# Moving the gain of the MLP's first norm from the rows of w_up to the transposed h, in a one-core decoder layer

## The chip, the core and the metric

The kernel runs on one core of one Trainium2 chip. The metric is the device time of one execution in microseconds (us). Besides DMA queues the core has five engines that matter here: PE (matmuls and transposes, which write to PSUM), ACT (ScalarE), DVE (VectorE), POOL (GpSimd) and SP (which issues most DMAs). Each engine works through its own queue in order, and waits on semaphores for the others.

## The reference

One decoder layer on x of 256 tokens by 2048 channels, in fp32. Two attention groups give `mixed`, and then:

```python
x = x + _rmsnorm(mixed @ w_out[layer], norm_attn_post[layer])

h = _rmsnorm(x, norm_mlp_pre[layer])
u = jnp.square(jax.nn.relu(h @ w_up[layer]))
x = x + _rmsnorm(u @ w_down[layer], norm_mlp_post[layer])
```

`_rmsnorm(x, gain)` divides each token's row by its root mean square and multiplies channel c by `gain[c]`. The gain of the MLP's first norm, `norm_mlp_pre`, multiplies the contraction index of `h @ w_up`; it can therefore be applied either to the channels of h or to the rows of w_up. w_up is 2048 x 8192 and w_down 8192 x 2048.

## The kernel before, in words

**Precision.** Every large matmul is done in three passes. An operand `a` is split into `hi` (a rounded to the matmul's format, written by an ACT copy) and `lo` (`a - hi`, written by DVE), and hi·hi + hi·lo + lo·hi is accumulated. `split` (L290) does this with an ACT copy and a DVE subtraction; `split_gain` (L296) does the same on `g * a`, where `g` is one number per partition: ACT takes it as its scale, DVE uses a SCALAR_TENSOR_TENSOR (multiply, then subtract) in place of a TENSOR_TENSOR. Both engines read the source, and DVE also reads the `hi` that ACT has just written.

**Tiling.** The contraction index lies on the 128 partitions, in tiles k of 128 rows. The tokens are two blocks b of 128. A weight tile is 128 x 1024 columns; it is loaded by DMA into one of five `raw` buffers and split into `hi` and `lo` (eight buffers each) several tiles ahead of its use (`Weights.emit`, L178). `wide_u` (L401) plans the tiles of w_up: 16 k-tiles for the first chunk of 1024 columns (j = 0), and for each of the seven further chunks 10 plain k-tiles and three pairs of k-tiles that are done in seven block products instead of eight, from sums of blocks of weights (`seven`, L333) and of h (`left_sums`, L958). The gains of the rows of w_up lie in `gcol`, one column per k-tile (columns 8 to 23). The plain k-tiles (16 + 7 x 10 = 86) are split with their column of `gcol`; the pairs are not multiplied by it, and there `left_sums` multiplies h instead.

**The stage around the change.** Out-projection (`acc_o`) ends with the fourth chunk of 512 columns, first for block b = 0, then for b = 1. When a block is finished, `residual(b)` (L832) runs beside the matmuls. It computes the token's scale (DVE, then POOL), updates x in four pieces of 512 channels on DVE (L841), and for each piece n lets PE transpose four 128 x 128 blocks into one PSUM tile `ht` (L847 to L849). The four `ht` tiles of a block take the two PSUM banks of `tp_bank` (L275) in turn, so that the third piece's transposes write the bank of the first, and the fourth's the bank of the second. Then `split` turns all four blocks of the PSUM tile at once into `hT_hi` and `hT_lo` (L853, one ACT and one DVE instruction of 128 x 512). After the four pieces x is sent to DRAM by a DMA on SP (L856), and ACT sums the squares of x (L860).

The matmuls of the first chunk of w_up (`acc_u`) begin while this is under way: k-tiles 0 to 6 for b = 0, then 0 to 6 for b = 1, then both blocks for each later k-tile. PE's queue holds them and the transposes in one fixed order. The order of all work is written out by `Flow`, a clock of assumed costs that decides between which matmuls each step of `residual` is placed; splits of weight tiles fall between the splits of h on ACT and DVE.

`left_sums` (L958) runs after that, for three pairs of k-tiles. It adds hT_hi and hT_lo, multiplies by the gain (L965), forms the block sums, and splits both the multiplied h (back into hT) and the sums.

Below, k-tiles of w_up in the first chunk are called k0, k1 and so on, and the pieces of h n0 to n3 of block b0 or b1.

## Time and profile before

| | us |
|---|---|
| median of three runs | 1053.56 (1052.34 to 1053.63) |
| profiled execution | 1052.05 |
| its span, first to last instruction | 1050.3 |
| PE busy in it | 1039.0 |
| DVE busy | 811.0 |
| ACT busy | 625.4 |
| POOL busy | 61.5 |

The span is what the profile sees between its first and last instruction; 1.75 us of the profiled execution's time lie around it. The views used are: the page's first part (busy time by engine), the list of waits of PE, groups of instructions by line and shape (count, busy time, mean duration), and the instructions of one engine in order of time. In such a time row the columns are start, duration, engine, line, operation, output <- inputs, shapes and count; a bracket at the end gives the idle time before it and what ended it. Durations of neighbours on one engine overlap a little (about 0.1 us on ACT and 0.06 to 0.1 on DVE), so the distance between starts is the time that an instruction costs its queue.

### The profile page before, as it was taken

The numbers are of one execution on the slowest core, as the hardware profiler recorded it, in microseconds if no ns is written. First come the engines' busy times: TensorE is split into PE (matmuls) and PEld (weight loads), VectorE is DVE, ScalarE is ACT, GpSimd is POOL, SyncE is SP. The second block draws the span as 40 slices with busy tenths as digits, with TensorE's granted clock in tenths as the row PEclk, the third lists the DMA queues.
The fourth block names the chain that finished last, engine by engine and source line by source line (L and its number), as shares of the span: only waits on it lengthen the run. The fifth ranks groups of instructions, "written<-read, shape, count | busy, mean of one in ns | idle before, by whom it ended". The sixth has DMA issues, their size and how long they took to land.

```text
span 1050.3 us, 13459 instructions
## 1 busy us (share of the span) xinstructions
PE 1039.0 (99%) x4854; PEld 865.9 (82%) x4854; DVE 811.0 (77%) x1080; ACT 625.4 (60%) x834; POOL 61.5 (6%) x116
## 2 busy tenths in 40 slices
PE   9999999999999999999999999999999999999996
PEld 6888899888888788888888888888888888888885
DVE  6676536577557679879888798887899978989995
ACT  6675436565555467666665666666567564766661
POOL 0000000000000000010000000000000001112100
PEclk9999999999999999999999999999999999999999
DMA  8975447454447295646556465469788767788952
GB/s 298 371 230 155 140 127 239 141 166 155 141 170 234 77 344 174 224 143 238 194 189 201 145 234 194 151 227 319 246 276 315 267 223 259 268 300 313 381 186 81
DMA packets 80643, 229.34 MB, mean 218 GB/s; under 512 B 7616, under 2 KB 12224, under 8 KB 80192
## 3 DMA queue, kind: packets, MB, share of 16 engines
q1 hardware_dynamic: 65888, 176.45, 50.3%
q0 software_dynamic: 14112, 51.39, 14.2%
q8 instruction: 38, 0.62, 0.2%
q10 hardware_dynamic: 576, 0.64, 0.2%
q14 instruction: 29, 0.24, 0.1%
HBM read 212.72 MB, written 15.73 MB: 218 GB/s over the span
## 4 chain that ended last, share of the span: by engine, by line
PE 96%; DVE 1%; DMA 1%; issue 1%; ACT 0%; POOL 0%; DVEq 0%; POOLq 0%; ACTq 0%
PE y L283 26%; PE acc_u L283 26%; PE acc_o L283 8%; PE m L283 5%; PE md L283 5%; PE acc_v L283 4%; PE acc_qk L283 4%; PE acc_ckv L283 2%; PE acc_ukv L283 2%; PE acc_q L283 2%; PE acc_cq L283 2%; PE acc_k L283 2%; PE acc_uq L283 2%; PE rt L287 1%; PE sc_b L283 1%
## 5 line engine op out<-in xcount | busy, mean ns | idle before, releaser
L294 DVE TENSOR_TENSOR lo<-raw,hi 128x1024 fp32r<-128x1024 f32 (+3 forms) x213 | 241.7, 1152 | 91.5 <-ACT hi L293 90.7
L293 ACT ACTIVATE hi<-raw 128x1024 fp32r<-128x1024 f32 (+3 forms) x213 | 209.5, 999 | 77.6 <-PE y L283 20.8
L283 PE MATMUL acc_u<-hi,hT_hi 128*128 128x512 f32 x386 | 153.3, 397 | 0.0
L283 PE MATMUL acc_u<-hi,hT_lo 128*128 128x512 f32 x386 | 151.0, 391 | 0.4 <-DVE hT_lo L294 0.4
L283 PE MATMUL acc_u<-lo,hT_hi 128*128 128x512 f32 x386 | 150.7, 391 | 0.0
L283 PE MATMUL y<-hi,uhi 128*128 128x512 f32 x376 | 146.8, 390 | 0.0
L283 PE MATMUL y<-hi,ulo 128*128 128x512 f32 x376 | 146.5, 390 | 0.0
L283 PE MATMUL y<-lo,uhi 128*128 128x512 f32 x376 | 146.5, 390 | 0.0
L298 DVE SCALAR_TENSOR_TENSOR lo<-raw,gcol,hi 128x1024 fp32r<-128x1024 f32 x86 | 107.6, 1280 | 11.2 <-ACT hi L297 11.0
L297 ACT ACTIVATE hi<-raw,gcol 128x1024 fp32r<-128x1024 f32 x86 | 97.8, 1151 | 24.8 <-PE acc_u L283 10.9
L283 PEld LDWEIGHTS acc_u<-hi,hT_lo 128*128 128x128 f32 x386 | 72.5, 188 | 16.1 <-DVE hT_lo L294 0.8
L283 PEld LDWEIGHTS acc_u<-lo,hT_hi 128*128 128x128 f32 x386 | 72.6, 188 | 14.2
L283 PEld LDWEIGHTS acc_u<-hi,hT_hi 128*128 128x128 f32 x386 | 72.6, 188 | 13.9
L283 PEld LDWEIGHTS y<-hi,uhi 128*128 128x128 f32 x376 | 70.6, 188 | 14.6
L283 PEld LDWEIGHTS y<-hi,ulo 128*128 128x128 f32 x376 | 70.6, 188 | 14.6
L283 PEld LDWEIGHTS y<-lo,uhi 128*128 128x128 f32 x376 | 70.6, 188 | 14.5
L283 PE MATMUL acc_o<-hi,mixT_hi 128*128 128x512 f32 x128 | 51.9, 405 | 0.0
L294 DVE TENSOR_TENSOR lo<-st_down,hi 128x1024 fp32r<-128x1024 f32 x40 | 48.1, 1220 | 4.0 <-ACT hi L293 3.8
L283 PE MATMUL acc_o<-hi,mixT_lo 128*128 128x512 f32 x128 | 50.2, 392 | 0.0
L283 PE MATMUL acc_o<-lo,mixT_hi 128*128 128x512 f32 x128 | 50.0, 391 | 0.0
L293 ACT ACTIVATE hi<-ab 128x512 fp32r<-128x512 f32 (+1 forms) x38 | 32.0, 842 | 29.3 <-PE acc_u L283 24.4
L293 ACT ACTIVATE hi<-st_down 128x1024 fp32r<-128x1024 f32 x40 | 42.1, 1053 | 11.1 <-PE y L283 9.5
(322 smaller groups left out, 1986.3 us busy)
## 6 DMA issues: line engine op xcount, KB each, us to landing
raw<-in_w_down SPq DMA_DIRECT2D x88, 512.0 KB, 6.0
raw<-in_w_up SPq DMA_DIRECT2D x86, 512.0 KB, 4.5
raw<-in_w_in SPq DMA_DIRECT2D x55, 512.0 KB, 5.0
ab<-in_w_up POOLq DMA_DIRECT2D x36, 512.0 KB, 5.0
raw<-in_w_out SPq DMA_DIRECT2D x32, 512.0 KB, 4.3
ab_down<-in_w_down POOLq DMA_DIRECT2D x20, 512.0 KB, 6.4
ukeep<-ulo SPq DMA_DIRECT2D x15, 512.0 KB, 7.2
ulo<-ukeep POOLq DMA_DIRECT2D x15, 512.0 KB, 5.4
```

What stands on the lines that cost most here:

```text
L283: nc.tensor.matmul(out, a, b, start=start, stop=stop)
L287: nc.tensor.transpose(out, a, ident)
L293: nc.scalar.activation(hi, src, AF.Copy)
L294: nc.vector.tensor_tensor(out=lo, in0=src, in1=hi.bitcast(F32), op=OP.subtract)
L297: nc.scalar.activation(hi, src, AF.Copy, scale=g)
L298: nc.vector.scalar_tensor_tensor(out=lo, in0=src, scalar=g, in1=hi.bitcast(F32), op0=OP.mult, op1=OP.subtract)
```

## The change

Three edits. The plain k-tiles of w_up are split without the gain. In `residual`, the split of one `ht` tile becomes four calls of `split_gain`, one for each of its k-tiles, with that k-tile's column of `gcol`. In `left_sums`, where h now carries the gain already, the multiplication and the second split of h are left out; only the block sums are split.

```diff
@@ wide_u @@
             if what == "k":
-                ts = [weights.plan(up_weight(j, k), 1, CW, gcol[:, 8 + k:9 + k])]
+                ts = [weights.plan(up_weight(j, k), 1, CW)]
@@ residual @@
             if n in (0, 1):
                 update((n + 2,))
-            split(hT[0][:, 4 * n:4 * n + 4, b * P:(b + 1) * P], hT[1][:, 4 * n:4 * n + 4, b * P:(b + 1) * P], tv)
+            for k in range(4 * n, 4 * n + 4):
+                split_gain(*[tok(x, k, b) for x in hT], tv[:, k - 4 * n], gcol[:, 8 + k:9 + k])
@@ left_sums @@
-        for i in range(2):
-            nc.vector.tensor_scalar_mul(f[:, i * S:(i + 1) * S], f[:, i * S:(i + 1) * S], gcol[:, 8 + k + i:9 + k + i])
         four_sums(q, f)
         st = [late["st"][:, i * 512:(i + 1) * 512] for i in (2 * kp, 2 * kp + 1)]
         yield 3.0
-        for t, x in ((hs, f), (st, q)):
-            nc.scalar.activation(t[0], x, AF.Copy)
+        nc.scalar.activation(st[0], q, AF.Copy)
         yield 1.5
-        for t, x in ((hs, f), (st, q)):
-            tt(out=t[1], in0=x, in1=t[0].bitcast(F32), op=OP.subtract)
+        tt(out=st[1], in0=q, in1=st[0].bitcast(F32), op=OP.subtract)
```

The order on PE, POOL and SP is the same in both kernels. What moves is seen on ACT and DVE in the stage of the splits of h. The rows below are the queue's order, with the semaphores that a row waits for in brackets; `ht` is the PSUM tile of transposes, `hi` and `raw` are weight tiles.

ACT's queue before, from the first split of b0 to the fourth:

```order
L293 ACTIVATE hT_hi<-ht_3222 128x4x128 [waits PE_49]
L297 ACTIVATE hi_3235<-raw_3233,gcol 128x1024 [waits DMAHW7_49,DVE_49]
L293 ACTIVATE hT_hi<-ht_3242 128x4x128 [waits PE_49]
L802 ACTIVATE junko_3253,ssy_2434<-acc_o_0_1_0_3094 128x512 [waits PE_49,Activation_49]
L297 ACTIVATE hi_3262<-raw_3260,gcol 128x1024 [waits DMAHW0_49,DVE_49]
L293 ACTIVATE hT_hi<-ht_3269 128x4x128 [waits PE_49]
```

The same place now:

```order
L297 ACTIVATE hT_hi<-ht_3222,gcol 128x128 [waits PE_49]
L297 ACTIVATE hT_hi<-ht_3222,gcol 128x128 [waits DVE_49] x3
L293 ACTIVATE hi_3241<-raw_3239 128x1024 [waits DMAHW7_49]
L297 ACTIVATE hT_hi<-ht_3248,gcol 128x128 [waits PE_49]
L297 ACTIVATE hT_hi<-ht_3248,gcol 128x128 [waits DVE_49] x3
L802 ACTIVATE junko_3265,ssy_2434<-acc_o_0_1_0_3094 128x512 [waits PE_49,Activation_49]
L293 ACTIVATE hi_3274<-raw_3272 128x1024 [waits DMAHW0_49]
```

One instruction became four in the same place, and the second to fourth of them wait for DVE, which no split of h did before.

DVE's queue before, from the splits of b0 to the first updates of x for b1:

```order
L294 TENSOR_TENSOR hT_lo<-ht_3222,hT_hi 128x4x128 [waits Activation_49]
L298 SCALAR_TENSOR_TENSOR lo_3236<-raw_3233,gcol,hi_3235 128x1024 [waits DMAHW7_49,Activation_49]
L841 SCALAR_TENSOR_TENSOR x_117<-yg_2861,rstd_post_3196,x_117 128x512
L294 TENSOR_TENSOR hT_lo<-ht_3242,hT_hi 128x4x128 [waits Activation_49]
L803 TENSOR_TENSOR yg_2862<-acc_o_0_1_0_3094,g_post 128x512 [waits Activation_49]
L298 SCALAR_TENSOR_TENSOR lo_3263<-raw_3260,gcol,hi_3262 128x1024 [waits DMAHW0_49,Activation_49]
L294 TENSOR_TENSOR hT_lo<-ht_3269,hT_hi 128x4x128 [waits Activation_49]
```

The same place now:

```order
L298 SCALAR_TENSOR_TENSOR hT_lo<-ht_3222,gcol,hT_hi 128x128 [waits Activation_49] x4
L294 TENSOR_TENSOR lo_3242<-raw_3239,hi_3241 128x1024 [waits DMAHW7_49,Activation_49]
L841 SCALAR_TENSOR_TENSOR x_117<-yg_2861,rstd_post_3196,x_117 128x512
L298 SCALAR_TENSOR_TENSOR hT_lo<-ht_3248,gcol,hT_hi 128x128 [waits Activation_49] x4
L803 TENSOR_TENSOR yg_2862<-acc_o_0_1_0_3094,g_post 128x512 [waits Activation_49]
L294 TENSOR_TENSOR lo_3275<-raw_3272,hi_3274 128x1024 [waits DMAHW0_49,Activation_49]
L298 SCALAR_TENSOR_TENSOR hT_lo<-ht_3281,gcol,hT_hi 128x128 [waits Activation_49] x4
```

Each of the four waits for its own ACT instruction; the updates of x and the splits of weights stand behind them in the queue, in the order of before.

## The prediction

> **What bounds the kernel now.** I read the page's busy times first, then the list of PE's waits.

> ```profile
> span 1050.3 us, 13459 instructions
> PE 1039.0 (99%) x4854; PEld 865.9 (82%) x4854; DVE 811.0 (77%) x1080; ACT 625.4 (60%) x834; POOL 61.5 (6%) x116
> ```

> ```profile
> PE acc_qk L283 <- ACT hi L293: 1.0, 2, 0.8
> PE acc_u L283 <- DVE hT_lo L294: 0.4, 1, 0.4
> ```

> PE is busy for 99% of the span, and after the first microseconds it waits for a split once: 0.4 us for `hT_lo`, in the stage that is changed. So time saved on ACT or DVE elsewhere has nothing to win, and what counts is whether the changed stage makes PE wait. Its rows on PE, in order of time:

> ```profile
> 354.86 0.60 PE L287 MATMUL ht<-ident,x 128*128 128x128 f32 x4
> 356.69 0.60 PE L287 MATMUL ht<-ident,x 128*128 128x128 f32 x4
> 361.94 0.39 PE L283 MATMUL acc_u<-hi,hT_hi 128*128 128x512 f32 x1
> 363.07 0.39 PE L283 MATMUL acc_u<-hi,hT_lo 128*128 128x512 f32 x1
> 363.35 0.42 PEld L287 LDWEIGHTS ht<-ident,x 128*128 128x128 f32 x4 [0.31 <-issue]
> 363.38 0.63 PE L287 MATMUL ht<-ident,x 128*128 128x128 f32 x4
> 366.72 0.50 PE L283 MATMUL acc_u<-hi,hT_lo 128*128 128x512 f32 x1 [0.40 <-DVE hT_lo L294]
> 367.75 0.60 PE L287 MATMUL ht<-ident,x 128*128 128x128 f32 x4
> 369.58 0.60 PE L287 MATMUL ht<-ident,x 128*128 128x128 f32 x4
> 379.57 0.39 PE L283 MATMUL acc_u<-hi,hT_hi 128*128 128x512 f32 x1
> ```

> These are the third and fourth transposes of b0, the first use of k5, the last matmul before b1's transposes, the first transposes of b1, the first use of b1's `hT_lo`, b1's third and fourth transposes, and k8. Matmuls start 0.23 us apart (363.07 would be followed at 363.30; the load row before b1's transposes shows 0.31 us of idle time, which ends as the first of the two updates of x at 362.48 does, half of 1.41 us later). The queues beside it, DVE, and then ACT with one DMA of SP:

> ```profile
> 352.47 0.69 DVE L294 TENSOR_TENSOR hT_lo<-ht,hT_hi 128x512 fp32r<-128x512 f32 x1 [1.25 <-ACT hT_hi L293]
> 353.51 1.28 DVE L298 SCALAR_TENSOR_TENSOR lo<-raw,gcol,hi 128x1024 fp32r<-128x1024 f32 x1 [0.35 <-ACT hi L297]
> 354.71 0.74 DVE L841 SCALAR_TENSOR_TENSOR x<-yg,rstd_post,x 128x512 f32<-128x512 f32 x1
> 355.38 0.68 DVE L294 TENSOR_TENSOR hT_lo<-ht,hT_hi 128x512 fp32r<-128x512 f32 x1
> 355.98 0.68 DVE L803 TENSOR_TENSOR yg<-acc_o,g_post 128x512 f32<-128x512 f32 x1
> 360.16 1.28 DVE L298 SCALAR_TENSOR_TENSOR lo<-raw,gcol,hi 128x1024 fp32r<-128x1024 f32 x1
> 362.48 1.41 DVE L841 SCALAR_TENSOR_TENSOR x<-yg,rstd_post,x 128x512 f32<-128x512 f32 x2 [0.67 <-POOL rstd_post L485]
> 365.98 0.68 DVE L294 TENSOR_TENSOR hT_lo<-ht,hT_hi 128x512 fp32r<-128x512 f32 x1
> ```

> ```profile
> 351.84 0.60 ACT L293 ACTIVATE hT_hi<-ht 128x512 fp32r<-128x512 f32 x1 [4.45 <-PE ht L287]
> 354.43 0.60 ACT L802 ACTIVATE junko<-acc_o 128x512 bf16<-128x512 f32 x1 [0.17 <-PE acc_o L283]
> 361.61 1.15 ACT L297 ACTIVATE hi<-raw,gcol 128x1024 fp32r<-128x1024 f32 x1 [1.03 <-DMA raw<-in_w_up]
> 355.91 0.39 SPq L175 DMA_DIRECT2D raw<-in_w_up  x1
> ```

> The stretch before b1 in sum (columns: length, then busy us of PE, PEld, DVE, ACT and POOL):

> ```profile
> 356.00:362.00 6.00, 6.00 (x30) 4.97 (x29) 5.77 (x9) 4.93 (x10) 0.11 (x1) 1.00 0.78 262
> ```

> DVE is busy for 5.77 of these 6 us, up to the chain that makes x of b1 (362.48), and that chain already holds PE for 0.3 us. Whatever is added to DVE's queue here goes straight to PE.

> **Price of the new splits.** The same code (`split_gain` out of a PSUM tile that holds several pieces) stands in the latents' part:

> ```profile
> 180.52 0.45 ACT L297 ACTIVATE mixT_hi<-ckvt,gcol 128x256 fp32r<-128x256 f32 x1
> 181.53 0.84 ACT L297 ACTIVATE mixT_hi<-ckvt,gcol 128x256 fp32r<-128x256 f32 x2 [0.55 <-DVE mixT_lo L298]
> ```

> ```profile
> 181.01 0.48 DVE L298 SCALAR_TENSOR_TENSOR mixT_lo<-ckvt,gcol,mixT_hi 128x256 fp32r<-128x256 f32 x1 [0.19 <-ACT mixT_hi L297]
> 182.03 0.88 DVE L298 SCALAR_TENSOR_TENSOR mixT_lo<-ckvt,gcol,mixT_hi 128x256 fp32r<-128x256 f32 x2 [0.54 <-ACT mixT_hi L297]
> ```

> The second ACT piece of a tile does not follow the first: it waits 0.55 us, until DVE has read the tile's first piece. The two engines alternate, 1.01 us for a pair (180.52 to 181.53). In the changed order the second to fourth piece of each `ht` wait for DVE just so. For the width of 128 I take the slopes of these groups (columns: count, busy us, mean ns):

> ```profile
> L298 DVE SCALAR_TENSOR_TENSOR lo<-raw,gcol,hi 128x1024 fp32r<-128x1024 f32 x86 | 107.6, 1280 | 11.2 <-ACT hi L297 11.0
> L298 DVE SCALAR_TENSOR_TENSOR mixT_lo<-ckvt,gcol,mixT_hi 128x256 fp32r<-128x256 f32 x4 | 1.8, 481 | 1.3 <-ACT mixT_hi L297 1.3
> L297 ACT ACTIVATE hi<-raw,gcol 128x1024 fp32r<-128x1024 f32 x86 | 97.8, 1151 | 24.8 <-PE acc_u L283 10.9 <-DMA raw<-in_w_up 6.7 <-PE acc_o L283 3.1
> L297 ACT ACTIVATE mixT_hi<-ckvt,gcol 128x256 fp32r<-128x256 f32 x4 | 1.8, 467 | 1.1 <-DVE mixT_lo L298 1.1
> L294 DVE TENSOR_TENSOR lo<-raw,hi 128x1024 fp32r<-128x1024 f32 x179 | 215.8, 1222 | 69.7 <-ACT hi L293 69.0
> L293 ACT ACTIVATE hi<-raw 128x1024 fp32r<-128x1024 f32 x179 | 186.6, 1055 | 56.9 <-PE y L283 20.8 <-DMA raw<-in_w_in 11.0 <-PE acc_o L283 5.5
> ```

> DVE: (1280 - 481) / 768 = 1.04 ns a column, so 481 - 133 = 0.35 us for 128. ACT: (1151 - 467) / 768 = 0.89, so 467 - 114 = 0.35; with 0.04 us for each hand-over (180.52 + 0.45 to 181.01) a pair is 0.79 us (0.36 + 0.35 + 0.08). A group of four takes 4 x 0.79 - 0.04 = 3.1 us from ACT's start to DVE's end, where before it was 1.32 (351.84 to 353.16), and DVE is held for 3 x 0.79 + 0.35 = 2.7 us, where it was 0.6 (355.38 to 355.98). Bounds: a pair is no dearer than the 256-wide one (1.01), and no cheaper than with both pieces at half of their 256-wide rows (0.23 + 0.24 + 0.08 = 0.55). I take 0.79, by the slopes of both rows, which leave 0.21 and 0.24 us that do not depend on the width.

> **The sum, on before's clock.** I carry ACT's and DVE's queues forward in the new order, with a weight split at 1.05 and 1.22 us (the plain rows above), and note where PE must wait.

> - b0 n0: ACT begins at 351.9, DVE ends at 355.0. PE's third transposes, due at 354.86, write the same bank: **+0.2**.
> - ACT splits k3 from 354.5 to 355.6, DVE to 356.8; x's update to 357.5; only then DVE takes n1, which ends at 357.4 + 2.7 = 360.15. PE's fourth transposes (356.69 + 0.2 = 356.9) need n1's bank: **+3.3**.
> - `junko`, k4's split and `yg` follow; n2 runs on DVE from 362.5 to 365.2. ACT splits k5 from 364.7 to 365.75, DVE to 367.0. PE wants k5 at 361.94 + 3.5 = 365.4: **+0.4** for `hi`, **+1.0** for `lo`.
> - n3 on DVE to 369.6. k6's `lo` begins at 370.25. From there to x's first update for b1 it took 362.48 - 360.16 = 2.3, so it begins at 372.45 and ends at 373.2. PE arrives at b1's transposes at 363.30 + 4.9 = 368.2: **+5.0**.
> - b1 n0: from that update to `hT_lo` it was 365.98 - 362.48 = 3.5, so DVE begins at 375.95 and k0's piece is there at 376.35. PE is due at 375.95: **+0.4**. Only a quarter is waited for here, which helps by 0.3 us.
> - n0's last piece ends at 378.7. PE's third transposes are due at 377.3: **+1.45**. Behind them x's update and n1, to 382.0; the fourth are due at 380.55: **+1.5**.
> - n2 and n3 of b1 end at 384.6 and 387.2. Nobody waits: their k-tiles come after k7. The split of k8 stands behind them and three sums of squares on ACT; its `lo` is ready at 391.55, PE uses it at 379.57 + 12.5 + 0.23 = 392.3. That is 0.75 us of cover; without it each further us of delay would be PE's.

> Together 0.2 + 3.3 + 1.4 + 5.0 + 0.4 + 1.45 + 1.5 = 13.25 us of waits, of which 0.3 + 0.4 were there before: **+12.5 us**. Carried forward with pairs of 1.01 us the same queues give +18, with 0.55 +8.

> **What I cost at nothing.** 86 weight splits become cheaper, by 1280 - 1222 = 58 ns on DVE (5.0 us) and 1151 - 1055 = 96 ns on ACT (8.3 us); `left_sums` loses two multiplications, one copy and one subtraction in each of three pairs. All of it lies beside matmuls that wait for none of it (the list of waits above), so no PE time comes back. In the stage itself the four cheaper splits are in the sum. On SP, the save of x and the load of k7's raw tile behind it slip with x's updates, by 2 us and for b1 by 12: k7's tile, asked for at 355.91 and split at 361.61, comes at about 363.7, and ACT now gets to it at 371.7; k8's, asked for at 379.8, comes by the same 5.7 us at 385.5, and ACT gets to it at 389.2. POOL and the order of DMAs are unchanged.

> The sum is made on a profiled execution of 1052.05 us (span 1050.3), 1.5 below the median of 1053.56. Added to the median: 1066.0 us.

> **The rivals.**

> *The pieces overlap* (no measurable change). The first input is split by pieces out of SBUF, and there they do follow each other:

> ```profile
> 13.35 1.31 ACT L297 ACTIVATE xT_hi<-xraw 128x256 fp32r<-128x256 f32 x3
> 14.11 1.27 DVE L298 SCALAR_TENSOR_TENSOR xT_lo<-xraw,xT_hi 128x256 fp32r<-128x256 f32 x3
> ```

> If `ht` went so, four pieces would cost DVE 4 x 0.27 = 1.1 in place of 0.6, four times 0.5 less four cheaper weight splits is 1.75 us up to x of b1, and k0's piece comes 0.3 earlier: +1.4 us, 1055. Against it stand the waits of the latents' rows, which differ by the source in PSUM, and the waits for DVE in the order.

> *Not slower.* The wait at 366.72 ends after a quarter of the split, and 0.3 us or a little more of it goes: 1053. That decides only if four pieces occupy DVE no longer than the one did, 0.15 us a piece; the 256-wide row takes 0.48.

> [...]

> **How the numbers follow.** About 0.2% (2 us) can be told from no change. Forecast 0.73; clock 0.21, likewise slower; overlap 0.05 (1055, within 0.2%); not slower 0.01, given to faster. So slower 0.94, same 0.05, faster 0.01. The range runs from a pair of 0.58 us (+8.5) to one of 0.88 (+14.4) with the clock's 2 us on top: 1062 to 1070, which leaves out the outer part of both bounds and the two small cases.

> **What would show it.** Right: ACT rows `hT_hi` 128x128 with idle before three of four, ended by DVE; a group near 3.1 us; PE waits of 3 and 5 us before `ht`, ending near 360 and 373; the rest of PE's list as it was; DVE's sum smaller by 5 us for weights with no gain in time. Wrong: pieces back to back on ACT; a price of a pair far from 0.79; k8's weights late, which would add waits past 390; a clock below 1.00 after 373.

## The result and the profile after

The changed kernel takes 1065.49 us (median of 4 runs, 1065.02 to 1065.99), the kernel before, in the runs beside it, 1052.95 (1051.72 to 1053.63). The ratio is 1.012, with a 95% interval of 1.0103 to 1.0138: 12.5 us slower. The prediction said 1066.0, which is +12.5 on the median of 1053.56 that the kernel before had then.

The profiled execution of the changed kernel has a time of 1065.31 us. Its page, span and busy times:

```profile
span 1063.5 us, 13481 instructions
...
PE 1043.9 (98%) x4854; PEld 869.2 (82%) x4854; DVE 808.1 (76%) x1095; ACT 622.7 (59%) x855; POOL 62.7 (6%) x116
```

DVE and ACT are busy for 2.9 and 2.7 us less than before (811.0 and 625.4), and the span is 13.2 us longer. PE does the same 4854 instructions in 4.9 us more busy time; the other 8.3 us are idle time. The list of PE's waits (sum, count, longest) has two lines that were not there:

```profile
PE ht L287 <- DVE x L841: 4.8, 1, 4.8
PE ht L287 <- DVE hT_lo L298: 4.3, 2, 3.0
```

The groups of the new splits and of the weight splits (busy us, mean ns, idle time ahead and what ended it):

```profile
L298 DVE SCALAR_TENSOR_TENSOR hT_lo<-ht,gcol,hT_hi 128x128 fp32r<-128x128 f32 x32 | 11.0, 349 | 11.5 <-ACT hT_hi L297 11.5
L297 ACT ACTIVATE hT_hi<-ht,gcol 128x128 fp32r<-128x128 f32 x32 | 11.4, 367 | 20.1 <-DVE hT_lo L298 15.2 <-PE ht L287 4.9
L294 DVE TENSOR_TENSOR lo<-raw,hi 128x1024 fp32r<-128x1024 f32 x265 | 318.1, 1221 | 85.2 <-ACT hi L293 84.5
```

DVE stands idle for 11.5 us between its 32 pieces, ACT for 15.2 us, each waiting on a semaphore for the other. The weight splits are the cheap kind, 1221 ns, and there are now 265 of them, 179 and the 86 that lost the gain.

ACT's rows of the first group, in order of time (start, duration, and in brackets the idle time ahead with what ended it):

```profile
352.77 0.37 ACT L297 ACTIVATE hT_hi<-ht,gcol 128x128 fp32r<-128x128 f32 x1 [4.45 <-PE ht L287]
353.56 0.37 ACT L297 ACTIVATE hT_hi<-ht,gcol 128x128 fp32r<-128x128 f32 x1 [0.42 <-DVE hT_lo L298]
...
355.14 0.37 ACT L297 ACTIVATE hT_hi<-ht,gcol 128x128 fp32r<-128x128 f32 x1 [0.42 <-DVE hT_lo L298]
```

The pieces come 0.79 us apart. In this execution the stage begins 0.93 us later than in the one before (352.77 against 351.84). The difference is made in the first 20 us, before anything that the change touches: from 5.7 to 9.1 us matmuls start 0.43 us apart in this execution, and mostly 0.23 in the one before; what causes this is open. Times of the prediction are compared after adding 0.93.

DVE's queue: the last piece of b0's first group and of its second, the first piece of its fourth group and the weight split behind that, x's first two updates for b1, and the `lo` of k8:

```profile
355.54 0.35 DVE L298 SCALAR_TENSOR_TENSOR hT_lo<-ht,gcol,hT_hi 128x128 fp32r<-128x128 f32 x1 [0.44 <-ACT hT_hi L297]
...
360.64 0.35 DVE L298 SCALAR_TENSOR_TENSOR hT_lo<-ht,gcol,hT_hi 128x128 fp32r<-128x128 f32 x1 [0.44 <-ACT hT_hi L297]
...
367.76 0.35 DVE L298 SCALAR_TENSOR_TENSOR hT_lo<-ht,gcol,hT_hi 128x128 fp32r<-128x128 f32 x1
...
371.06 1.23 DVE L294 TENSOR_TENSOR lo<-raw,hi 128x1024 fp32r<-128x1024 f32 x1 [0.59 <-ACT hi L293]
...
373.32 1.42 DVE L841 SCALAR_TENSOR_TENSOR x<-yg,rstd_post,x 128x512 f32<-128x512 f32 x2 [0.67 <-POOL rstd_post L485]
...
390.71 1.23 DVE L294 TENSOR_TENSOR lo<-raw,hi 128x1024 fp32r<-128x1024 f32 x1 [2.72 <-ACT hi L293]
```

From the first piece of a group to the weight split behind it DVE's queue takes 371.06 - 367.76 = 3.30 us. Before it was 0.60 (the split at 355.38, the next instruction at 355.98). Part of the 3.30 is the 0.59 us at its end: ACT had been held by the pieces too, so its half of the weight split was not there yet. The experiments use this number, the price of a group on DVE's queue.

PE's rows: b0's fourth transposes with some of the matmuls behind them, and b1's first, third and fourth transposes:

```profile
361.05 1.12 PE L287 MATMUL ht<-ident,x 128*128 128x128 f32 x4 [3.04 <-DVE hT_lo L298]
...
362.39 0.63 PE L283 MATMUL acc_u<-lo,hT_hi 128*128 128x512 f32 x1
362.82 0.63 PE L283 MATMUL acc_u<-hi,hT_lo 128*128 128x512 f32 x1
...
364.10 0.41 PE L283 MATMUL acc_u<-hi,hT_lo 128*128 128x512 f32 x1
364.34 0.40 PE L283 MATMUL acc_u<-hi,hT_hi 128*128 128x512 f32 x1
...
374.13 0.95 PE L287 MATMUL ht<-ident,x 128*128 128x128 f32 x4 [4.82 <-DVE x L841]
...
379.53 0.66 PE L287 MATMUL ht<-ident,x 128*128 128x128 f32 x4
...
382.80 0.66 PE L287 MATMUL ht<-ident,x 128*128 128x128 f32 x4 [1.22 <-DVE hT_lo L298]
```

From before's 369.58 to 382.80 b1's fourth transposes moved by 13.22 us; less the 0.93 that is 12.3. PE meets no further wait in this stage, so this is the loss. But after both long waits PE is slow: matmuls come 0.43 us apart (362.39 to 362.82), where they came 0.23 apart before. The two stretches, with the granted clock in the third column from the right:

```profile
362.00:368.00 6.00, 6.00 (x23) 4.74 (x23) 3.92 (x7) 2.71 (x7) 0.00 (x0) 0.82 0.30 105
374.00:380.00 6.00, 5.87 (x25) 4.65 (x25) 4.66 (x11) 2.43 (x7) 0.98 (x1) 0.72 0.00 1
```

The kernel before, in the stretch with its b1's first transposes (363.38), has a clock of 1.00:

```profile
362.00:368.00 6.00, 5.60 (x30) 4.15 (x29) 5.41 (x9) 3.21 (x7) 1.42 (x2) 1.00 0.00 0
```

So the sum came out while one of the rivals, the fall of the clock, happened too. How both can be true is what the second half of the experiments is about.

### The profile page after: what moved, and what is told of

The parts are those of the page before. It is cut to its first block, busy times and chain, and to the rows that moved or that the text cites. A ratio compares the mean times of both kernels' runs of the same rounds, so it can differ in the third digit from the quotient of the medians.

```text
span 1063.5 us, 13481 instructions
## 1 busy us (share of the span) xinstructions
PE 1043.9 (98%) x4854; PEld 869.2 (82%) x4854; DVE 808.1 (76%) x1095; ACT 622.7 (59%) x855; POOL 62.7 (6%) x116
## 4 chain that ended last, share of the span: by engine, by line
PE 95%; DVE 2%; ACT 1%; issue 1%; DMA 0%; POOL 0%; DVEq 0%; POOLq 0%; ACTq 0%
PE y L283 25%; PE acc_u L283 25%; PE acc_o L283 8%; PE m L283 5%; PE md L283 5%; PE acc_qk L283 4%; PE acc_v L283 4%; PE acc_ckv L283 2%; PE acc_q L283 2%; PE acc_ukv L283 2%; PE acc_cq L283 2%; PE acc_k L283 2%; PE acc_uq L283 2%; PE rt L287 1%; PE sc_b L283 1%; DVE lo L294 1%
## 5 line engine op out<-in xcount | busy, mean ns | idle before, releaser
L294 DVE TENSOR_TENSOR lo<-raw,hi 128x1024 fp32r<-128x1024 f32 (+3 forms) x299 | 344.0, 1171 | 107.5 <-ACT hi L293 106.8
L293 ACT ACTIVATE hi<-raw 128x1024 fp32r<-128x1024 f32 (+3 forms) x299 | 299.3, 1016 | 104.3 <-PE y L283 20.8
L283 PE MATMUL acc_u<-hi,hT_hi 128*128 128x512 f32 x386 | 154.3, 400 | 0.0
L283 PE MATMUL acc_u<-lo,hT_hi 128*128 128x512 f32 x386 | 151.5, 393 | 0.0
L283 PE MATMUL acc_u<-hi,hT_lo 128*128 128x512 f32 x386 | 151.5, 393 | 0.0
L283 PE MATMUL y<-hi,uhi 128*128 128x512 f32 x376 | 146.6, 390 | 0.0
L283 PE MATMUL y<-hi,ulo 128*128 128x512 f32 x376 | 146.3, 389 | 0.0
L283 PE MATMUL y<-lo,uhi 128*128 128x512 f32 x376 | 146.3, 389 | 0.0
L283 PEld LDWEIGHTS acc_u<-hi,hT_lo 128*128 128x128 f32 x386 | 73.0, 189 | 15.5
L283 PEld LDWEIGHTS acc_u<-lo,hT_hi 128*128 128x128 f32 x386 | 73.2, 190 | 14.5
L283 PEld LDWEIGHTS acc_u<-hi,hT_hi 128*128 128x128 f32 x386 | 73.1, 189 | 14.2
L283 PEld LDWEIGHTS y<-hi,uhi 128*128 128x128 f32 x376 | 70.6, 188 | 14.7
L283 PEld LDWEIGHTS y<-hi,ulo 128*128 128x128 f32 x376 | 70.6, 188 | 14.7
L283 PEld LDWEIGHTS y<-lo,uhi 128*128 128x128 f32 x376 | 70.6, 188 | 14.5
L283 PE MATMUL acc_o<-hi,mixT_hi 128*128 128x512 f32 x128 | 51.8, 405 | 0.0
L294 DVE TENSOR_TENSOR lo<-st_down,hi 128x1024 fp32r<-128x1024 f32 x40 | 48.0, 1219 | 4.0 <-ACT hi L293 3.8
L293 ACT ACTIVATE hi<-ab 128x512 fp32r<-128x512 f32 (+1 forms) x38 | 32.0, 843 | 31.8 <-PE acc_u L283 29.7
L283 PE MATMUL acc_o<-hi,mixT_lo 128*128 128x512 f32 x128 | 50.2, 392 | 0.0
L283 PE MATMUL acc_o<-lo,mixT_hi 128*128 128x512 f32 x128 | 50.0, 390 | 0.0
L293 ACT ACTIVATE hi<-st_down 128x1024 fp32r<-128x1024 f32 x40 | 42.1, 1053 | 11.1 <-PE y L283 9.5
L283 PE MATMUL m<-hi,st 128*128 128x512 f32 x126 | 45.6, 389 | 0.0
L294 DVE TENSOR_TENSOR lo<-ab,hi 128x512 fp32r<-128x512 f32 (+1 forms) x38 | 35.2, 953 | 10.9 <-ACT hi L293 10.9
```

The costliest lines, as they stand in the source:

```text
L283: nc.tensor.matmul(out, a, b, start=start, stop=stop)
L293: nc.scalar.activation(hi, src, AF.Copy)
L294: nc.vector.tensor_tensor(out=lo, in0=src, in1=hi.bitcast(F32), op=OP.subtract)
```

## The experiments

The theory: ACT and DVE take turns at a PSUM tile, so a split in four pieces holds DVE's queue (and ACT's) several times as long, x of b1 and the free bank come late, and PE waits. Rivals: the gain in the instruction is what costs; the cheaper weights would win something if the cut were not in the way; the clock accounts for a part of the 12.5 us. The cut alone, the gain without the cut, ACT's four pieces first and the changed kernel with PE kept busy ran on one chip, with the kernel before at 1052.90 us (19 runs); the other four ran on another, with 1053.19 (9 runs).

**The cut alone.** The kernel before, with h split in four pieces, and the gain left on the rows of `w_up`:

```diff
-            split(hT[0][:, 4 * n:4 * n + 4, b * P:(b + 1) * P], hT[1][:, 4 * n:4 * n + 4, b * P:(b + 1) * P], tv)
+            for k in range(4 * n, 4 * n + 4):
+                split(*[tok(x, k, b) for x in hT], tv[:, k - 4 * n])
```

> The kernel before with one edit: each transposed tile of h is split in four pieces of 128 columns, without a gain; the gain stays on the rows of w_up. Theory 1 (ACT and DVE take turns on the pieces of one PSUM tile): a pair costs about 0.65 us here (0.28 on ACT and 0.29 on DVE by the plain 256-wide rows less 128 columns, and two hand-overs), so a group about 2.5 us; the queues carried forward give +10.5 to +12 us over before, that is 1063.5 to 1065. Theory 2 (the gain is what costs: the SCALAR_TENSOR_TENSOR and the ACT scale from gcol, or the weights that are no longer multiplied): within 1 us of before.

Measured: 1064.47 us (1064.16 to 1065.42), ratio 1.0107 (1.0092 to 1.0122), +11.6. Its ACT rows, and then its DVE rows for b0's fourth group and the weight split behind it:

```profile
353.45 0.28 ACT L293 ACTIVATE hT_hi<-ht 128x128 fp32r<-128x128 f32 x1 [4.45 <-PE ht L287]
354.08 0.28 ACT L293 ACTIVATE hT_hi<-ht 128x128 fp32r<-128x128 f32 x1 [0.36 <-DVE hT_lo L294]
```

```profile
367.42 0.28 DVE L294 TENSOR_TENSOR hT_lo<-ht,hT_hi 128x128 fp32r<-128x128 f32 x1
...
370.36 1.28 DVE L298 SCALAR_TENSOR_TENSOR lo<-raw,gcol,hi 128x1024 fp32r<-128x1024 f32 x1 [0.75 <-ACT hi L297]
```

Without any gain in the pieces the same alternation stands there, 0.64 us a pair (353.45 to 354.08) in place of 0.79, and 2.94 us a group. The cut by itself costs most of the 12.5 us; the gain in the pieces adds some 0.15 us a pair. The cheaper weights give some of that back: the idle time ahead of the weight split is 0.59 us in the changed kernel and 0.75 here.

**The gain without the cut.** The changed kernel with h split whole; the norm's gain is then nowhere:

```diff
-            for k in range(4 * n, 4 * n + 4):
-                split_gain(*[tok(x, k, b) for x in hT], tv[:, k - 4 * n], gcol[:, 8 + k:9 + k])
+            split(hT[0][:, 4 * n:4 * n + 4, b * P:(b + 1) * P], hT[1][:, 4 * n:4 * n + 4, b * P:(b + 1) * P], tv)
```

> The changed kernel with h split whole, as before. It leaves the gain of the MLP's first norm out altogether. It shows what the cheaper weight splits and the shorter left_sums are worth alone. Theory 1 (PE waits for none of them): 0 to -0.5 us against before, the 0.4 us wait for b1's first hT_lo a little shorter. Rival (the 5 us of DVE and 8 us of ACT come back in part, and the loss in the stage of h is larger than the difference of the two kernels): -2 us or more.

Measured: 1052.37 us (10 runs), ratio 0.9993 (0.9984 to 1.0002), which is not to be told from no change. The first lines of its list of PE's waits:

```profile
PE warm L505 <- DVE zero L502: 1.2, 1, 1.2
PE acc_qk L283 <- ACT hi L293: 0.5, 1, 0.5
```

The stage makes PE wait no longer, not even the 0.4 us of before. That is all there is to win: 86 weight splits cheaper by 58 ns on DVE and 96 ns on ACT buy about 0.5 us by the medians; the interval reaches from none to 1.7 us.

**The same arithmetic, ACT's four pieces first.** The changed kernel with two loops in place of one:

```diff
-            for k in range(4 * n, 4 * n + 4):
-                split_gain(*[tok(x, k, b) for x in hT], tv[:, k - 4 * n], gcol[:, 8 + k:9 + k])
+            ks = range(4 * n, 4 * n + 4)
+            for k in ks:
+                nc.scalar.activation(tok(hT[0], k, b), tv[:, k - 4 * n], AF.Copy, scale=gcol[:, 8 + k:9 + k])
+            for k in ks:
+                nc.vector.scalar_tensor_tensor(
+                    out=tok(hT[1], k, b), in0=tv[:, k - 4 * n], scalar=gcol[:, 8 + k:9 + k],
+                    in1=tok(hT[0], k, b).bitcast(F32), op0=OP.mult, op1=OP.subtract)
```

> The changed kernel with the same eight instructions for each transposed tile, but ACT's four ahead of DVE's four, so that ACT waits for DVE in none of them and DVE only for ACT's last. Theory 1 (turns on one PSUM tile): ACT's four take 4 x 0.27 us, DVE's four 4 x 0.27 after them; the queues carried forward give PE waits of 0.5 us at the fourth transposes of b0, 1.3 at the first of b1 and 0.4 at its first hT_lo, +1.4 us over before, 1054.4. Theory 2 (four small instructions cost more than one large one, in whatever order): as the changed kernel, +12 us.

Measured: 1053.72 us (10 runs), ratio 1.0006 (0.9996 to 1.0015), +0.8. One ACT row, DVE's rows for the fourth group and the weight split behind it, and its two waits of PE in the stage:

```profile
351.67 1.14 ACT L855 ACTIVATE hT_hi<-ht,gcol 128x128 fp32r<-128x128 f32 x4 [4.45 <-PE ht L287]
```

```profile
360.61 1.12 DVE L857 SCALAR_TENSOR_TENSOR hT_lo<-ht,gcol,hT_hi 128x128 fp32r<-128x128 f32 x4
361.65 1.21 DVE L294 TENSOR_TENSOR lo<-raw,hi 128x1024 fp32r<-128x1024 f32 x1
```

```profile
PE ht L287 <- DVE x L841: 1.1, 1, 1.1
...
PE ht L287 <- DVE hT_lo L857: 0.2, 1, 0.2
```

Four pieces in a row take ACT 1.14 us and DVE 1.12, with no idle time between them (the profile joins them, x4). The group costs DVE's queue 1.04 us instead of 3.30, ACT runs ahead so that the weight split finds its `hi` ready, and nearly the whole loss is gone. The instructions are the changed kernel's, in number, size and operands; only their order differs. So it is not their durations that cost, but the waiting for each other.

**Two PSUM tiles for a group.** The changed kernel with four transposes spread over two banks, and the pieces taken from them in turn:

```diff
-            t = tp_bank(f"ht{n}{b}")
+            t = [tp_bank(f"ht{n}{b}"), at_bank(f"hu{n}{b}")]
             for k in range(4):
-                transpose(t[:, k * P:(k + 1) * P], xs[b][:, n * 512 + k * P:n * 512 + (k + 1) * P])
-            tv = t.rearrange("p (k s) -> p k s", k=4)
+                transpose(t[k // 2][:, k * P:(k + 1) * P], xs[b][:, n * 512 + k * P:n * 512 + (k + 1) * P])
+            tv = [x.rearrange("p (k s) -> p k s", k=4) for x in t]
...
-            for k in range(4 * n, 4 * n + 4):
-                split_gain(*[tok(x, k, b) for x in hT], tv[:, k - 4 * n], gcol[:, 8 + k:9 + k])
+            for i in (0, 2, 1, 3):
+                k = 4 * n + i
+                split_gain(*[tok(x, k, b) for x in hT], tv[i // 2][:, i], gcol[:, 8 + k:9 + k])
```

> The changed kernel with the four transposes of a piece of h in two PSUM tiles (two banks), two in each, and split_gain called in the order 0, 2, 1, 3, so that consecutive pieces lie in different tiles. Everything else, all eight instructions too, as in the changed kernel. If the turns are taken on one PSUM tile: ACT works on one tile while DVE reads the other, a group takes about 2 us in place of 3.1, and the queues carried forward give +4.2 us over before (waits of 0.4 at b0's fourth transposes and 3.7 at b1's first), plus up to 1 us for the clock: 1057 to 1058. If ACT and DVE took turns for another reason (the shared hT tiles, gcol), +12 us as in the changed kernel.

Measured: 1057.87 us (1057.62 to 1058.69), ratio 1.005 (1.0036 to 1.0063), +4.7. Its ACT rows, and DVE's first piece of the fourth group with the weight split behind it:

```profile
351.25 0.37 ACT L297 ACTIVATE hT_hi<-ht,gcol 128x128 fp32r<-128x128 f32 x1 [4.24 <-PE ht L287]
351.51 0.36 ACT L297 ACTIVATE hT_hi<-hu,gcol 128x128 fp32r<-128x128 f32 x1
352.04 0.37 ACT L297 ACTIVATE hT_hi<-ht,gcol 128x128 fp32r<-128x128 f32 x1 [0.16 <-DVE hT_lo L298]
```

```profile
362.28 0.34 DVE L298 SCALAR_TENSOR_TENSOR hT_lo<-ht,gcol,hT_hi 128x128 fp32r<-128x128 f32 x1
...
364.26 1.23 DVE L294 TENSOR_TENSOR lo<-raw,hi 128x1024 fp32r<-128x1024 f32 x1 [0.59 <-ACT hi L293]
```

A piece from the other tile starts 0.26 us after the last (351.25 to 351.51), with no wait; the wait comes only where the first tile is read again. It is the shared tile that makes the engines take turns, and not the tiles of `hT` or `gcol`, which the pieces share here as in the changed kernel. Each tile has a PSUM bank of its own, so tile and bank are not told apart. ACT waits 0.42 us for DVE from piece to piece of one tile in the changed kernel, and not at all from one tile to the other here. No run here shows what two reads at once would do.

Before looking at the clock, the ways beside each other. The second column is the price of a group on DVE's queue (start of the weight split behind b0's fourth group less the start of its first piece; for the kernel before 360.16 - 359.56). Totals differ ahead of the stage too, so the last column counts the stage alone, in the one execution traced of each kernel: from the start of b0's first transposes to that of b1's fourth, less the same in the kernel before (369.58 - 351.20 = 18.38):

| kernel | group on DVE, us | PE's wait for x, us | time against before, us | stage in the trace against before, us |
|---|---|---|---|---|
| before, whole | 0.60 | 0.3 | 0 | 0 |
| ACT's four first | 1.04 | 1.1 | +0.8 | +1.2 |
| two plain pieces (below) | 1.91 | 3.6 | +5.8 | +5.2 |
| two tiles | 1.98 | 3.5 | +4.7 | +6.2 |
| plain pieces, no gain | 2.94 | 4.3 | +11.6 | +10.5 |
| changed kernel | 3.30 | 4.8 | +12.5 | +12.3 |

The stage follows the price of the group from row to row. The medians do so but for the two in the middle, which are 1.1 us apart the other way. In their traces the reversal lies ahead of the stage: b0's first transposes start at 352.77 with two pieces and at 350.83 with two tiles, and the difference is there after the first 20 us. PE also waits for b0's second group, ahead of the fourth transposes: 0.2 us with ACT's four first and with two tiles, 0.6 with two pieces, 2.35 with the plain cut and 3.04 in the changed kernel.

**Cut for b0 only.** The kernel before with four plain pieces for b0 and a whole split for b1:

```diff
-            split(hT[0][:, 4 * n:4 * n + 4, b * P:(b + 1) * P], hT[1][:, 4 * n:4 * n + 4, b * P:(b + 1) * P], tv)
+            for k in range(4 * n, 4 * n + 4, 4 if b else 1):
+                e = k + (4 if b else 1)
+                split(*[x[:, k:e, b * P:(b + 1) * P] for x in hT], tv[:, k - 4 * n:e - 4 * n])
```

> The kernel before with four plain pieces for b0 alone; b1 is split whole, as before. By the queues carried forward b0 alone makes the waits of 2.7, 1.4 and 4.8 us and gives +8.8 us, so that b1's own pieces are the smaller part; the lower clock after the wait of 4.8 us has only 0.8 us of waits behind it, so up to 0.9 us more: 1061.7 to 1062.7. If the pieces of either block cost the same, about half of the four-piece kernel's 11.6: 1058.7.

Measured: 1063.14 us (1062.83 to 1063.23), ratio 1.0098 (1.0084 to 1.0112), +9.95. PE's waits in the stage:

```profile
PE ht L287 <- DVE x L841: 4.3, 1, 4.3
PE ht L287 <- DVE hT_lo L294: 2.4, 1, 2.4
```

Of the 11.6 us of the plain cut 9.95 arise from b0's four groups, though the longest wait stands at b1's transposes: it is b0's pieces that hold DVE ahead of x's update. Against before it came out 0.25 us over the upper end of what was expected (+9.7). The two intervals overlap, so the 1.7 us that are left for b1's own groups are rough. In the traces the stage is only 0.3 us shorter than with all eight groups cut (+10.2 against +10.5). The traced execution of the plain cut has in addition a wait of 0.85 us at 459.20, far behind the stage, for a sum on DVE (L1009); no other list of waits has it, and what causes it is open.

**PE kept busy in the long waits.** The changed kernel with matmuls of zeros into an idle bank (11 ahead of b0's fourth transposes, 18 ahead of b1's first):

```diff
+            for _ in range({(0, 3): 11, (1, 0): 18}.get((b, n), 0)):
+                nc.tensor.matmul(late["wb"], zero[:, :P], zero, start=True, stop=True)
             for k in range(4):
                 transpose(t[:, k * P:(k + 1) * P], xs[b][:, n * 512 + k * P:n * 512 + (k + 1) * P])
...
+                late["wb"] = bank(6, "warm2")
```

> The changed kernel with matmuls on zeros into an idle PSUM bank in PE's queue: 11 ahead of b0's fourth transposes, 18 ahead of b1's first, so that PE idles under 1 us in either wait and does the same work otherwise. In the changed kernel the matmuls after both waits start 0.43 us apart for 3 us instead of 0.23. Theory 1 (what PE loses at the lower clock is taken from waits that follow at once): the granted clock stays at 1.00, waits of about 1.4 us at k5 and 1.5 at b1's third transposes come back, and the time is that of the changed kernel within 0.7 us. Rival (the lower clock adds to the time): 1.5 to 3 us less than the changed kernel.

Measured: 1064.88 us (1064.10 to 1065.87), ratio 1.011 (1.0093 to 1.0127), +12.0. The clock in the two stretches (third column from the right) and the waits that PE now meets:

```profile
362.00:368.00 6.00, 5.15 (x22) 3.70 (x21) 3.90 (x7) 2.57 (x7) 0.00 (x0) 1.00 0.21 87
374.00:380.00 6.00, 4.75 (x26) 3.45 (x26) 4.66 (x11) 2.13 (x7) 0.98 (x1) 1.00 0.01 1
```

```profile
367.60 0.51 PE L283 MATMUL acc_u<-lo,hT_hi 128*128 128x512 f32 x1 [0.76 <-DVE lo L294]
...
379.22 0.66 PE L287 MATMUL ht<-ident,x 128*128 128x128 f32 x4 [1.16 <-DVE hT_lo L298]
...
382.50 0.65 PE L287 MATMUL ht<-ident,x 128*128 128x128 f32 x4 [1.23 <-DVE hT_lo L298]
```

The clock stays at 1.00 and the time moves by 0.6 us, within the spread of the runs; the stage takes 30.64 us here and 30.66 in the changed kernel. What PE gains by the full clock it spends waiting: 0.76 us for k5's `lo` and 1.16 us ahead of b1's third transposes, two waits that the changed kernel does not have. DVE's queue, and not PE, sets when this stage ends, so with these waits behind it the slower PE of the changed kernel cost 0.02 us in the stage.

**Two pieces, and the same with PE kept busy.** To see the fall of the clock where no waits follow: the kernel before with two plain pieces of 256, and then 13 matmuls of zeros ahead of b1's first transposes in addition (the second diff).

```diff
-            split(hT[0][:, 4 * n:4 * n + 4, b * P:(b + 1) * P], hT[1][:, 4 * n:4 * n + 4, b * P:(b + 1) * P], tv)
+            for k in (4 * n, 4 * n + 2):
+                split(*[x[:, k:k + 2, b * P:(b + 1) * P] for x in hT], tv[:, k - 4 * n:k - 4 * n + 2])
```

```diff
+            for _ in range(13 if (b, n) == (1, 0) else 0):
+                nc.tensor.matmul(late["wb"], zero[:, :P], zero, start=True, stop=True)
```

> The kernel before with each transposed tile of h split in two pieces of 256 columns, without a gain (the gain stays on the rows of w_up). One turn between ACT and DVE in place of three. The plain 256-wide rows (0.38 on ACT, 0.42 on DVE) make a group of 1.7 us; the queues carried forward give PE waits of 0.8 at b0's fourth transposes and 3.7 at b1's first, +4.6 us over before, if PE runs at full clock. The wait of 3.7 us is long enough for the clock to fall as it did after a wait of 2.35 us with four pieces. Here nearly no wait follows that could take up the loss (0.5 us at b1's first hT_lo), so if the lower clock costs what PE then does not do, +1.0 us comes on top: 1058.5 in place of 1057.5.

> The two-piece kernel with 13 matmuls on zeros into an idle PSUM bank ahead of b1's first transposes, so that PE idles 0.7 us there in place of 3.7 and does the same work otherwise. If the lower clock costs time where no wait follows: 0.7 to 1.3 us less than the two-piece kernel, with the granted clock at 1.00 throughout. If it costs nothing here either: the same time.

Measured: two pieces 1059.02 us (1058.32 to 1060.27), ratio 1.0062 (1.0049 to 1.0074), +5.8; with the zeros 1057.95 (1056.50 to 1058.22), ratio 1.0045 (1.0032 to 1.0059), +4.8. The wait for x and the stretch behind it, for two pieces:

```profile
PE ht L287 <- DVE x L841: 3.6, 1, 3.6
```

```profile
368.00:374.00 6.00, 4.46 (x18) 3.83 (x19) 4.87 (x9) 3.17 (x8) 1.53 (x2) 0.72 0.00 1
```

And with the zeros:

```profile
PE ht L287 <- DVE x L841: 0.8, 1, 0.8
```

```profile
368.00:374.00 6.00, 5.11 (x28) 3.62 (x27) 5.10 (x10) 2.83 (x8) 1.35 (x2) 1.00 0.01 1
```

Here the clock counts: 1.1 us between the medians, as expected, and 0.9 us in the traces, all of it from b1's first transposes to its third (5.00 us against 4.10). The two intervals overlap, so the size is not settled beyond "about 1 us".

No kernel here beats the one before; splitting whole without the gain, which is no longer the same computation, shows that there are some 0.5 us to be had by the medians.

## Why the prediction was right, and where it was not

**The price of a pair: right.** 0.79 us was worked out from the slopes of two widths; 352.77 to 353.56 is 0.79. ACT's piece took 0.37 (0.36 by the prediction), DVE's 0.35 (0.35). A group from ACT's start to DVE's end is 355.54 + 0.35 - 352.77 = 3.1 us, as said. That the pieces alternate, and that this is the shared PSUM tile's doing, the plain cut, ACT's four first and the two tiles have shown; the rival that they overlap has fallen.

**The long waits: right in place and nearly in size.** b0's third transposes, due at 354.86 + 0.93 = 355.79, start at 355.95: 0.16 us for the 0.2. b0's fourth transposes were to start at 360.2, with the 0.93 at 361.1: 361.05. b1's first at 373.2, so 374.13: 374.13. b1's third at 378.7, so 379.63: 379.53. b1's fourth at 382.0, so 382.93: 382.80. The waits ahead of the first two were to be 3.3 and 5.0 us and are 3.04 and 4.82.

**The short waits between: wrong, in a way that cancels.** The terms 0.4 + 1.0 (k5), 0.4 (b1's first `hT_lo`) and 1.45 (b1's third transposes) are not in the trace: no such wait is listed. They were worked out for a PE at full speed. PE ran at a granted clock of 0.50 behind each long wait (361 to 364 and 375 to 377 us) and came late by itself, by about 1.4 us at k5 and as much at b1's second transposes, which the third follow. That is worked out from the rows. From b0's fourth transposes to the sixth matmul behind them PE took 3.05 us (361.05 to 364.10); at full clock it is 0.41 + 0.32 + 4 x 0.23 = 1.65 (the steps between starts behind the same transposes in the plain cut, before its clock fell). And b1's second transposes came 3.31 us after the first (374.13 to 377.44), where before it was 1.87 (363.38 to 365.25). With PE kept busy, two of the waits came back at 0.76 and 1.16 us. So the sum held because it was DVE's queue that was carried forward, and when PE is late for it or waits for it is the same.

**The clock rival: it happened, and cost next to nothing here.** The forecast gave a fall of PE's clock a chance of 0.21 and put 2 us for it on top of the range; no run shows these 2 us. What the runs show: the granted clock fell to 0.50 in the wait of 3.04 us at b0's fourth transposes, just behind that of 4.82 us at b1's first, and behind one of 2.35 us in the plain cut (below). The run with PE kept busy puts the net cost of this in the changed kernel at 0.6 us by the medians and 0.02 in the stage, not distinguishable from none; two pieces, without the zeros and with them, are 1.1 us apart. In the changed kernel the waits behind took the loss up: 0.76 and 1.16 us of them are there with PE kept busy and are not without. The chance for the fall of the clock was far too low.

**What was costed at nothing: right.** The weights' savings are there on DVE (107.6 + 215.8 = 323.4 us before, 318.1 now) and on ACT, and give no time; splitting whole without the gain, which keeps all of them, gives 0.5 us with an interval that includes none. k8's `lo` ends at 390.71 + 1.23 = 391.94, by the prediction 391.55 + 0.93 = 392.5, and PE does not wait for it. The slip of the raw tiles on SP cost nothing either: no wait of PE behind 382.80 follows from it.

## What to carry to other kernels

Here a PSUM tile is read by two engines, and cutting its reads into four pieces turned one hand-over into many: from piece to piece ACT waited 0.42 us for DVE and DVE 0.44 us for ACT, and the price of a group on DVE's queue went from 0.60 to 3.30 us. Let one engine read all its pieces first (1.04 here), or put alternate pieces in different tiles (1.98 here, each tile in a bank of its own). Price such a change by how long it holds the queue of the engine that feeds the bound, up to the next thing that PE waits for, and not by the sum of its instructions. Busy time saved beside a PE that is 98 to 99% busy is worth nothing unless PE waits for it: 86 weight splits cheaper by 58 ns on DVE and 96 ns on ACT gave 0.5 us by the medians, with an interval that includes none. And the clock that fell in a wait cost only what the waits behind it did not take up: here nothing that could be measured in the changed kernel, and about 1 us with two pieces.

## What the runs showed of the hardware that was not expected

```profile
360.81 0.66 PE L287 MATMUL ht<-ident,x 128*128 128x128 f32 x4 [2.35 <-DVE hT_lo L294]
```

The granted clock of that kernel in stretches of 1 us (third column from the right):

```profile
361.00:362.00 1.00, 1.00 (x7) 0.87 (x7) 0.69 (x1) 1.00 (x3) 0.00 (x0) 1.00 1.14 262
362.00:363.00 1.00, 1.00 (x4) 0.80 (x3) 0.92 (x1) 0.22 (x2) 0.00 (x0) 0.54 0.74 184
363.00:364.00 1.00, 1.00 (x3) 0.76 (x3) 0.66 (x3) 0.28 (x1) 0.00 (x0) 0.50 1.03 422
...
365.00:366.00 1.00, 1.00 (x5) 0.82 (x4) 0.29 (x1) 1.00 (x2) 0.00 (x0) 0.75 0.00 0
366.00:367.00 1.00, 1.00 (x6) 0.82 (x5) 0.78 (x1) 0.36 (x2) 0.00 (x0) 1.00 0.00 0
```

PE resumes at a clock of 1.00, is busy for more than a microsecond (360.81 to 362.1), and only then falls to 0.50, for some 3.4 us (362.1 to 365.5, worked out from the 0.54 and the 0.75 of the stretches at the two ends). The fall did not come at PE's return, but in the changed kernel once ahead of it and once behind: within the wait of 3.04 us (clock 0.85 from 360 to 361 us, PE back at 361.05), and after the wait of 4.82 us only when PE had been back for 0.2 us (1.00 from 373 to 374, 0.68 from 374 to 375, PE back at 374.13). Nor was it always 3.4 us long: with two tiles, where PE waited 3.5 us, it was 6.8 us (365.9 to 372.7, worked out from means of 0.82 from 362 to 368 and 0.61 from 368 to 374, with a clock of either 1.00 or 0.50). Waits of 0.8, 1.1 and 1.23 us, in the runs with two pieces and zeros, with ACT's four first and with the changed kernel's PE kept busy, left the clock at 1.00 in the stretches of 6 us that hold them. No run had a wait between 1.23 and 2.35 us in this stage, and whether the fall depends on when the wait comes was not tried.
